# Both score maps of a differential attention at once, each on half the rows of TensorE's array

## The chip, the core and the metric

The kernel runs on one NeuronCore of a Trainium2 chip. Its engines work side by side, each through its own list of instructions: TensorE (PE) multiplies matrices, and its weight loads are listed apart as PEld; VectorE is DVE, ScalarE is ACT, GpSimd is POOL; SyncE (SP) issues most of the loads. The metric is the device time of one execution in microseconds (us). Before the change three runs gave 3132.48, 3139.52 and 3141.57 us; the median is 3139.52 us.

TensorE multiplies a stationary operand, loaded into the array beforehand (up to 128 rows by 128 columns), with a moving operand that streams through it one column after another. The rows of the array are the index that is summed over. Every matrix product of this kernel loads its own stationary operand; the trace lists that load (LDWEIGHTS) and the product (MATMUL) apart. Products add up in PSUM.

## The reference

One layer of a decoder for a prompt of 2048 tokens and for 8 sample tokens: a normed input projection; a pooling mixer and a differential attention side by side; an output projection; cross attention into 256 memory tokens; a gated feed-forward with a short convolution; a final norm. All is float32. The change is in the prompt's differential attention, four heads, where each head has two maps c of 64 dimensions:

```
s = jnp.einsum('bqhcd,bkhcd->bhcqk', q, k) * (DIFF_HD ** -0.5)          # DIFF_HD = 64
s = jnp.where(dist >= 0, s + bias, -jnp.inf)                             # bias: -slope of the head * distance
a = jax.nn.softmax(s, axis=-1)
w = a[:, :, 0] - lam * a[:, :, 1]                                        # the two maps
o = jnp.einsum('bhqk,bkhe->bqhe', w, v)
```

## The kernel before

**Precision.** TensorE takes its operands in fp32r, which keeps fewer bits than float32. So nearly every operand is split into a high and a low part (hi, lo), and a product is built from hi by hi, hi by lo and lo by hi, three products that accumulate in PSUM.

**Stages.** The prompt is cut into four chunks of 512 tokens (the last carries the 8 sample rows too). The work is written as a list of items; `weave` spreads one list among another by estimated times, and the framework that builds the program then sets the order of instructions on every engine, with semaphores for what depends on what. The attention of chunks 0 and 1 (`att01`) is woven into the input projection of chunks 2 and 3; the attention of chunks 2 and 3 (`att23`) is woven with the output projection, the cross attention of chunk 0 and some work on the memory. Feed-forward fills the rest of the program.

**Attention.** A `Unit` is one head's 128 queries, 64 units in all. Unit i of a head (0 to 15) has (i + 1) * 128 keys. They are taken in halves of at most 1024 keys, so units 0 to 7 have one half and units 8 to 15 two. `scores(c, hf)` handles one map and one half: it takes a PSUM tile of 1024 columns from a pool of two (`PA`), fills it by products of at most 512 columns (line 1057), and VectorE then reads it, adds the distances and keeps the running minimum (line 1068, tile T out of sc). ScalarE takes the exponentials (line 1075), `combine` and `combine2` form the difference of the maps (lines 1084 to 1092), `turn` transposes it on TensorE (line 1098, wT), and `av` multiplies it with the values (line 1109, O). The steps of three successive units are mixed: scores of unit i, combination of i - 1, transposes and values of i - 2.

**Operands of the scores.** `k_evac` splits a chunk's keys into kh and kl (128 rows each: 64 of map 0, 64 of map 1) and stores them in DRAM by map: for map c, the 64 rows of kh above the 64 rows of kl. `att_load` brings one such tile K[c][hf] of 128 rows for each map and half. `att_q` brings, for each map, the high and the low queries, each of them twice, in rows 0 to 63 and again in rows 64 to 127, by four loads. So one product over all 128 rows gives qh by (kh + kl), a second ql by (kh + kl): two products a map, four for both.

Of the kernel before, what the change touches and what calls it, by code (L numbers as in the profile page):

```python
# [20 lines left out]
P = 128  # L21
# [25 lines left out]
def tile_trunk_step(ctx: ExitStack, tc: tile.TileContext, a, o):  # L47
# [142 lines left out]
    def rstd_v(ss, p, n, scale, eps):  # L190
        """as rstd, on the vector engine alone: a first guess from the exponent's bits, and three steps of Newton's"""
        v_, y, t = Tn("rv"), tp.tile([P, 8], I32, tag="t", name="ri"), Tn("rt")
        v_, y, t = v_[:p, :n], y[:p, :n], t[:p, :n]
        V.tensor_scalar(v_, ss, scale, eps, ALU.mult, ALU.add)
        V.tensor_scalar(y, v_.bitcast(I32), 1, None, ALU.logical_shift_right)
        V.tensor_scalar(y, y, -1, 0x5F3759DF, ALU.mult, ALU.add)
        y = y.bitcast(F32)
        for _ in range(3):
            V.scalar_tensor_tensor(t, y, -0.5, v_, ALU.mult, ALU.mult)
            V.tensor_tensor(t, t, y, ALU.mult)  # L200
            V.scalar_tensor_tensor(y, t, 1.5, y, ALU.add, ALU.mult)
        return y
# [13 lines left out]
    def norm_steps(c, x, g0, name, done, spill=None, rs=None):  # L216
        """items that norm the chunk x (4 tiles, in place), spill x to DRAM, and split the result"""
# [63 lines left out]
    class Weight:  # L281
        """a weight tile of 1024 columns in k parts, as loaded or as its high and low parts"""
# [19 lines left out]
    def cols(name, c0):  # L302
        """n-tile of 128 columns of a [1024, N] weight: [128, 8 kt, 128]"""
        return lambda: Weight(a[name][0, :, c0:c0 + P].rearrange("(k p) n -> p k n", p=P), 8)
# [11 lines left out]
    def item(specs, fn, cost=0.0, lat=0.0):  # L316
        """a piece of work: the weight tiles that it takes, the tensor engine's time in it, and how long what
        follows it in its own list has to wait"""
        return (specs, fn, cost, max(lat, cost, 0.3))

    def steps(specs, fn, cost, n):
        """fn's work, a generator, as n items"""
        st = {}

        def part(i):
            def run(ws):
                if i == 0:
                    st["g"] = fn(ws)
                next(st["g"], None)
                if i == n - 1:  # L330
                    for _ in st["g"]:
                        pass
            return run

        return [item(specs if i == 0 else [], part(i), cost / n) for i in range(n)]

    def weave(main, extra, lo=0.0, hi=1.0):
        """extra's items spread over main's span [lo, hi], both kept in order, by their times"""
        tm, te = sum(i[2] for i in main) or 1.0, sum(i[3] for i in extra) or 1.0
        out, k, dm, de = [], 0, 0.0, 0.0  # L340
        for i in main:
            out.append(i)
            dm += i[2]
            while k < len(extra) and lo + (hi - lo) * (de / te) <= dm / tm:
                out.append(extra[k])
                de += extra[k][3]
                k += 1
        return out + extra[k:]

    def in_turn(parts):  # L350
        """each one's four parts (load, split, product, turn), the load ahead by one and the turn behind by one"""
        out = [parts[0][0]]
        for b, p in enumerate(parts):
            out += [q[0] for q in parts[b + 1:b + 2]] + [p[1]] + ([parts[b - 1][3]] if b else []) + [p[2]]
        return out + [parts[-1][3]]

    def merge(x, y):
        """x's and y's items in one list, as long as the longer of the two"""
        tx, ty = sum(i[3] for i in x), sum(i[3] for i in y)
        both_, n = [], max(tx, ty)  # L360
        for z, t in ((x, tx), (y, ty)):
            at = 0.0
            for i in z:
                both_.append((at / t, i))
                at += i[3]
        both_.sort(key=lambda e: e[0])
        ends = [e[0] for e in both_[1:]] + [1.0]
        return [i[:3] + ((end - at) * n,) for (at, i), end in zip(both_, ends)]
# [4 lines left out]
    def later(dt, fn, key=None):  # L373
        """fn is traced when dt more of the tensor engine's time has been, or when its key is needed"""
        pending.append((clock[0] + dt, fn, key))
# [20 lines left out]
    def drive(items):  # L396
        """runs items in order; the weights of later ones are loaded ahead[0] tiles before their use, and their high
        and low parts taken ahead[1] and ahead[2] tiles before it"""
# [23 lines left out]
    def proj(c, hs, w, name):  # L422
        """[128 n, tokens of chunk c] of an n-tile; hs = (hi, lo) of the chunk, w = (hi, lo) [128, 8, 128]"""
# [271 lines left out]
    def k_evac(c, h, view):  # L695
# [6 lines left out]
        for cc in range(2):  # L702
            for z, t in enumerate((kh, kl)):
                ST.dma_start(k_d[c // 2][h][cc, z * HD:(z + 1) * HD, t0:t0 + CH], f(t[cc * HD:(cc + 1) * HD, :CH]))
# [228 lines left out]
    def sample_av(b):  # L933
# [27 lines left out]
        def fn3(_):  # L961
# [5 lines left out]
            # row (z, h) of head h's columns  # L967
# [43 lines left out]
    def att_load(h, nhf, old):  # L1011
        def fn(_):
            K = [[None, None] for _ in range(2)]
            Vt = [None, None]
            for hf in range(nhf):
                for c in range(2):
                    K[c][hf] = H("K", F32R)
                    SY.dma_start(f(K[c][hf][:, :1024]), k_d[hf][h][c])
# [5 lines left out]
    def att_q(qc, h):  # L1024
        def fn(_):
            q = [H("Q", F32R) for _ in range(2)]
            for c in range(2):
                for half in range(2):
                    SY.dma_start(f(v3(q[c], 2)[half * HD:(half + 1) * HD]),
                                 q_d[qc][:, h, c * HD:(c + 1) * HD, :].rearrange("z p t -> p z t"))  # L1030
# [3 lines left out]
    class Unit:  # L1034
        """a head's 128 queries"""
# [11 lines left out]
        def scores(self, c, hf):  # L1047
            def fn(_):
                if c == 0 and hf == 0:
                    self.l, self.mn = Tn("l"), [Tn("mn"), Tn("mn")]  # L1050
                Q, K = att["Q", self.qc, self.h], att[self.key][0]
                k0, m = self.halves[hf]
                ps = PA("sc")
                pc = [(0, m)] if m <= 512 else [(0, m // 2), (m // 2, m // 2)]
                for j, (c0, w) in enumerate(pc):
                    for z in range(2):
                        PE.matmul(ps[:, j * 512:j * 512 + w], v3(Q[c], 2)[:, z, self.t * P:(self.t + 1) * P],  # L1057
                                  K[c][hf][:, c0:c0 + w], start=z == 0, stop=z == 1)
                tl = H("T")
                d0 = 1920 - self.i * P + k0  # L1060
                if len(pc) == 1:
                    pin, out, din = ps[:, :m], tl[:, :m], Dt[:, d0:d0 + m]
                else:
                    pin = ps[:, :].rearrange("p (a b) -> p a b", a=2)[:, :, :m // 2]
                    out = tl[:, :m].rearrange("p (a b) -> p a b", a=2)
                    din = Dt[:, d0:d0 + m].rearrange("p (a b) -> p a b", a=2)
                mn = self.mn[c]
                V.tensor_tensor_reduce(out, pin, din, -SLOPE[self.h], 3.0e38 if hf == 0 else mn[:, 0:1], ALU.add, ALU.min,  # L1068
                                       mn[:, hf:hf + 1])
                self.T[c].append(tl)  # L1070
                last = len(self.halves) - 1
                if hf == last:
                    for g, (_, mg) in enumerate(self.halves):
                        tg = self.T[c][g]
                        S.activation(tg[:, :mg], tg[:, :mg], AF.Exp, bias=mn[:, last:last + 1], scale=-1.0,  # L1075
                                     accum_out=self.l[:, 2 * g + c:2 * g + c + 1])
            return item([], fn, self.halves[hf][1] / 512 * 0.43)
# [34 lines left out]
        def a_steps(self):  # L1112
            return [self.scores(c, hf) for c in range(2) for hf in range(len(self.halves))]
# [38 lines left out]
    def att_items(qcs):  # L1152
# [10 lines left out]
        for i in range(len(units) + 2):  # L1163
# [4 lines left out]
            if A:  # L1168
                k = 2 if len(A) > 2 else 1
                seq = A[:k] + B[:1] + A[k:] + B[1:]  # L1170
# [140 lines left out]
    sco = cp.tile([P, KT, NS], F32, name="sco")  # L1311

    def both(key, name, src, write):
        """items: rows of the samples (high parts over low ones) times a [1024, 1024] weight, by its quarters"""
# [66 lines left out]
    def sc_av(b):  # L1381
# [25 lines left out]
        def fn3(_):  # L1407
# [5 lines left out]
            # row (z, h) of head h's columns, which are tiles 2 h and 2 h + 1  # L1413
# [106 lines left out]
    def tail_down(nt, xx):  # L1520
        """the last chunk's squares and first half of its rows, as its tiles become final"""
# [128 lines left out]
    def raw_open(_):  # L1650
        """the distances' table gives its place to weights as they are loaded"""
# [52 lines left out]
```

## Time and profile before

| | us |
|---|---|
| median of the three runs | 3139.52 (3132.48 to 3141.57) |
| profiled execution, first to last instruction (span) | 3141.1 |
| TensorE busy with products (PE) | 3018.7 (96%) |
| TensorE busy with weight loads (PEld) | 2611.7 (83%) |
| VectorE busy | 2011.3 (64%) |
| ScalarE busy | 1403.9 (45%) |
| GpSimd busy | 530.8 (17%) |
| products of the scores, 640 | 172.9 busy, 386 ns each on the mean |

The profile is one execution of its own, listed by its span alone; no time around the span is shown for it. Busy times of TensorE need care: a product's listed duration goes from its start to the end of its results, and several are in the pipe at once, so what a product costs the engine is read from the distance between the starts of two neighbours, not from its duration. A weight load is listed beside the product that runs before it.

The scores run from 296 to 1043 us of the span. In that stretch TensorE is shared with the input projection (z, v), the output projection (wo), cross attention (S, vo) and the attention's own transposes and values.

### The profile page before, as it was taken

The numbers are of one execution on the slowest core, as the hardware profiler recorded it, in microseconds if no ns is written. First come the engines' busy times: TensorE is split into PE (matmuls) and PEld (weight loads), VectorE is DVE, ScalarE is ACT, GpSimd is POOL, SyncE is SP. The second block draws the span as 40 slices with busy tenths as digits, with TensorE's granted clock in tenths as the row PEclk, the third lists the DMA queues.
The fourth block names the chain that finished last, engine by engine and source line by source line (L and its number), as shares of the span: only waits on it lengthen the run. The fifth ranks groups of instructions, "written<-read, shape, count | busy, mean of one in ns | idle before, by whom it ended". The sixth has DMA issues, their size and how long they took to land.

```text
span 3141.1 us, 45513 instructions
## 1 busy us (share of the span) xinstructions
PE 3018.7 (96%) x17694; PEld 2611.7 (83%) x17694; DVE 2011.3 (64%) x3241; ACT 1403.9 (45%) x2214; POOL 530.8 (17%) x905
## 2 busy tenths in 40 slices
PE   7999999998999988999999999999999999999998
PEld 6789899887898877887777878887787777899998
DVE  5715654568667577757775546647767667866566
ACT  4625444446655444534443334534444344443342
POOL 0134234211111135302400000000013100010000
PEclk9999999899999999999999999999999999999999
DMA  8646356442632635434536432342455544343321
GB/s 272 189 150 226 102 163 190 148 138 64 206 107 85 212 117 161 157 117 137 161 105 213 148 109 94 112 150 92 163 175 207 166 144 169 121 142 96 94 81 71
DMA packets 378204, 451.98 MB, mean 144 GB/s; under 512 B 18321, under 2 KB 292248, under 8 KB 377972
## 3 DMA queue, kind: packets, MB, share of 16 engines
q1 hardware_dynamic: 336925, 349.29, 35.1%
q0 software_dynamic: 27264, 89.03, 8.2%
q10 hardware_dynamic: 13798, 10.76, 1.1%
q8 instruction: 139, 2.28, 0.3%
q14 instruction: 78, 0.63, 0.1%
HBM read 364.57 MB, written 84.85 MB: 143 GB/s over the span
## 4 chain that ended last, share of the span: by engine, by line
PE 82%; DVE 9%; DMA 3%; issue 2%; ACT 2%; POOL 1%; SPq 0%; DVEq 0%; ACTq 0%; POOLq 0%
PE up L429 19%; PE down L1503 13%; PE up L432 10%; PE z L443 8%; PE wo L443 6%; PE O L1109 3%; PE sc L1057 3%; DVE wlo L297 2%; PE vo L94 2%; PE vo L96 2%; PE vo L95 2%; PE S L94 2%; PE S L96 1%; PE S L95 1%; PE wT L1098 1%
## 5 line engine op out<-in xcount | busy, mean ns | idle before, releaser
L297 DVE TENSOR_TENSOR wlo<-wraw,whi 128x1024 fp32r<-128x1024 f32 x432 | 529.6, 1240 | 71.0 <-ACT whi L294 62.4
L429 PE MATMUL up<-h3hi,wlo 128*128 128x512 f32 (+1 forms) x1760 | 562.6, 352 | 7.7 <-ACT cc L1457 3.4
L429 PE MATMUL up<-h3hi,whi 128*128 128x512 f32 (+1 forms) x1760 | 559.6, 351 | 0.0
L294 ACT CAST whi<-wraw 128x1024 fp32r<-128x1024 f32 x432 | 443.1, 1048 | 238.4 <-DMA wraw<-in_w_up_dram 58.1
L1503 PE MATMUL down<-act,whi 128*128 128x512 f32 (+1 forms) x1760 | 449.8, 353 | 13.7 <-DVE xf L1510 13.2
L1463 DVE SCALAR_TENSOR_TENSOR cc<-Uf,vec,cc 128x512 f32<-128x512 f32 x176 | 135.0, 767 | 365.3 <-ACT cc L1457 353.3
L432 PE MATMUL up<-h3lo,whi 128*128 128x512 f32 (+1 forms) x1760 | 357.6, 349 | 0.0
L429 PEld LDWEIGHTS up<-h3hi,wlo 128*128 128x128 f32 x1760 | 308.4, 189 | 55.5 <-ACT cc L1457 3.9
L1456 ACT COPY Uf<-up 128x512 f32<-128x512 f32 (+1 forms) x176 | 103.6, 589 | 554.9 <-PE up L432 543.7
L429 PEld LDWEIGHTS up<-h3hi,whi 128*128 128x128 f32 x1760 | 308.4, 189 | 44.9
L1503 PEld LDWEIGHTS down<-act,whi 128*128 128x128 f32 x1760 | 293.5, 189 | 61.5 <-DVE xf L1510 17.4
L432 PEld LDWEIGHTS up<-h3lo,whi 128*128 128x128 f32 x1760 | 285.5, 188 | 46.8
L1503 PE MATMUL down<-act,wlo 128*128 128x512 f32 (+1 forms) x880 | 280.7, 352 | 3.5 <-DVE wlo L297 3.5
L1462 POOL COPY halo<-Uf 128x2 f32<-128x2 f32 x176 | 54.3, 308 | 1355.5 <-ACT Uf L1456 1355.3
L1510 DVE TENSOR_TENSOR xf<-xf,down 128x512 f32<-128x512 f32 (+1 forms) x308 | 206.7, 683 | 76.5 <-PE down L1503 75.0
L1075 ACT ACTIVATE T<-T,mn 128x1024 f32<-128x1024 f32 (+4 forms) x192 | 171.9, 897 | 128.3 <-DVE mn L1068 122.5
L1057 PE MATMUL sc<-K,Q 128*128 128x512 f32 (+5 forms) x640 | 172.9, 386 | 12.9 <-DVE mn L1068 12.6
L1068 DVE CUSTOM_DVE_ANT_0 T<-sc,Dt 128x1024 f32<-128x1024 f32 (+7 forms) x128 | 125.8, 985 | 86.1 <-PE sc L1057 83.5
L1503 PEld LDWEIGHTS down<-act,wlo 128*128 128x128 f32 x880 | 154.5, 189 | 29.3 <-DVE wlo L297 5.9
L443 PE MATMUL z<-h1hi,wlo 128*128 128x512 f32 (+1 forms) x480 | 158.4, 363 | 4.4 <-DVE pps L668 4.4
L1087 POOL TENSOR_SCALAR T<-T,rc 128x1024 f32<-128x1024 f32 (+4 forms) x96 | 92.4, 970 | 371.1 <-DVE rc L1085 194.4
L443 PE MATMUL z<-h1hi,whi 128*128 128x512 f32 (+1 forms) x480 | 153.8, 353 | 0.0
(420 smaller groups left out, 5994.2 us busy)
## 6 DMA issues: line engine op xcount, KB each, us to landing
wraw<-in_w_up_dram SPq DMA_DIRECT2D x176, 512.0 KB
wraw<-in_w_down_dram SPq DMA_DIRECT2D x88, 512.0 KB
wraw<-in_w_in_dram SPq DMA_DIRECT2D x32, 512.0 KB
Q<-q_d SPq DMA_DIRECT2D x64, 256.0 KB
wraw<-in_w_out_dram SPq DMA_DIRECT2D x32, 512.0 KB
wraw<-m_d SPq DMA_DIRECT2D x32, 512.0 KB
wraw<-vo_d SPq DMA_DIRECT2D x32, 512.0 KB
K<-k_d SPq DMA_DIRECT2D x24, 512.0 KB
```

Source lines behind the costliest of these rows:

```text
L94: PE.matmul(out, lh, rl, start=first, stop=False)
L294: S.copy(self.hi[:, :1024], self.raw[:, :1024])
L297: V.tensor_tensor(self.lo[:, :1024], self.raw[:, :1024], f(self.hi[:, :1024]), ALU.subtract)
L429: PE.matmul(out, w[wi][:, kt, :], kslice(hi, kt, c0, n), start=kt == 0 and wi == 1, stop=False)
L432: PE.matmul(out, w[0][:, kt, :], kslice(lo, kt, c0, n), start=False, stop=kt == KT - 1)
L443: PE.matmul(out, w[wi][:, kt, :], kslice(z, kt, c0, n), start=i == 0, stop=i == 3 * KT - 1)
L1057: PE.matmul(ps[:, j * 512:j * 512 + w], v3(Q[c], 2)[:, z, self.t * P:(self.t + 1) * P], K[c][hf][:, c0:c0 + w], start=z == 0, stop=z == 1)
L1068: V.tensor_tensor_reduce(out, pin, din, -SLOPE[self.h], 3.0e38 if hf == 0 else mn[:, 0:1], ALU.add, ALU.min, mn[:, hf:hf + 1])
L1075: S.activation(tg[:, :mg], tg[:, :mg], AF.Exp, bias=mn[:, last:last + 1], scale=-1.0, accum_out=self.l[:, 2 * g + c:2 * g + c + 1])
L1463: V.scalar_tensor_tensor(cc[:, :CH], U[:, 1:1 + CH], vc(CWT + FT + nt), cc[:, :CH], ALU.mult, ALU.add)
L1503: PE.matmul(out, ws[p][wi][:, nt, :], act[:, z + c0:z + c0 + n], start=st_ and p == 0, stop=en and p == 1)
L1510: V.tensor_tensor(sv(xx, c), sv(xx, c), view, ALU.add)
```

## The change

The scores of both maps are now one item, `scores(hf)`. It takes both PSUM tiles of the pool at once. For each piece of at most 512 columns it makes six products in place of four: low keys by high queries, high keys by high queries, high keys by low queries, each for map 0 (array rows 0 to 63) and map 1 (array rows 64 to 127) in alternation. Low by low, which the products over 128 rows included, is left out. Keys and queries stay as they are split: K[z][hf] holds the high (z = 0) or the low (z = 1) keys of both maps in 128 rows, and the query tile Q holds each row once. `k_evac` stores with two issues instead of four, `att_q` loads with one instead of four. The item's estimated time, which `weave` uses, is 0.7 us per 512 columns for both maps, where it was 0.43 for each. With half as many items, `att_items` cuts the list after the first one.

```diff
 def k_evac(c, h, view):
-        for cc in range(2):
-            for z, t in enumerate((kh, kl)):
-                ST.dma_start(k_d[c // 2][h][cc, z * HD:(z + 1) * HD, t0:t0 + CH], f(t[cc * HD:(cc + 1) * HD, :CH]))
+        for z, t in enumerate((kh, kl)):
+            ST.dma_start(k_d[c // 2][h][z, :, t0:t0 + CH], f(t[:, :CH]))
...
 def att_load(h, nhf, old):
-                for c in range(2):
-                    K[c][hf] = H("K", F32R)
-                    SY.dma_start(f(K[c][hf][:, :1024]), k_d[hf][h][c])
+                for z in range(2):
+                    K[z][hf] = H("K", F32R)
+                    SY.dma_start(f(K[z][hf][:, :1024]), k_d[hf][h][z])
...
 def att_q(qc, h):
-            q = [H("Q", F32R) for _ in range(2)]
-            for c in range(2):
-                for half in range(2):
-                    SY.dma_start(f(v3(q[c], 2)[half * HD:(half + 1) * HD]),
-                                 q_d[qc][:, h, c * HD:(c + 1) * HD, :].rearrange("z p t -> p z t"))
+            q = H("Q", F32R)
+            SY.dma_start(f(v3(q, 2)), q_d[qc][:, h].rearrange("z p t -> p z t"))
...
-        def scores(self, c, hf):
+        def scores(self, hf):
-                ps = PA("sc")
+                ps = [PA("sc"), PA("sc")]
                 pc = [(0, m)] if m <= 512 else [(0, m // 2), (m // 2, m // 2)]
                 for j, (c0, w) in enumerate(pc):
-                    for z in range(2):
-                        PE.matmul(ps[:, j * 512:j * 512 + w], v3(Q[c], 2)[:, z, self.t * P:(self.t + 1) * P],
-                                  K[c][hf][:, c0:c0 + w], start=z == 0, stop=z == 1)
-                tl = H("T")
+                    for zq, zk in ((0, 1), (0, 0), (1, 0)):
+                        for c in range(2):
+                            rows_ = slice(c * HD, (c + 1) * HD)
+                            PE.matmul(ps[c][:, j * 512:j * 512 + w], Q[rows_, zq, self.t * P:(self.t + 1) * P],
+                                      K[zk][hf][rows_, c0:c0 + w], start=zk == 1, stop=zq == 1)
...
-            return item([], fn, self.halves[hf][1] / 512 * 0.43)
+                for c in range(2):
+                    tl = H("T")
...
+            return item([], fn, self.halves[hf][1] / 512 * 0.7)
...
 def a_steps(self):
-            return [self.scores(c, hf) for c in range(2) for hf in range(len(self.halves))]
+            return [self.scores(hf) for hf in range(len(self.halves))]
...
 def att_items(qcs):
-                k = 2 if len(A) > 2 else 1
-                seq = A[:k] + B[:1] + A[k:] + B[1:]
+                seq = A[:1] + B[:1] + A[1:] + B[1:]
```

What stands on TensorE in the new program is not simply the order of that loop, because the framework orders the instructions. Two places show it. In these rows a tile's number tells the PSUM tile: an item of the new program has two sc tiles, the first for map 0 (array rows 0 to 63), the second for map 1 (rows 64 to 127).

TensorE in the first part of the attention (head 0, unit 3, one piece of 512 columns), before; z is the input projection of chunk 3:

```order
L443 MATMUL z_3022<-h1hi_2822,whi_2655 128x260 x2
L1057 MATMUL sc_3057<-K_2641,Q_2647 128x512 x2
L443 MATMUL z_3022<-h1hi_2882,wlo_2659 128x260 x2
...
L96 MATMUL pool_3084<-phi_3010,pws_921 128x512
L1057 MATMUL sc_3091<-K_2643,Q_2648 128x512 x2
L443 MATMUL z_3022<-h1lo_2764,whi_2655 128x260 x4
```

The same place in the new program:

```order
L443 MATMUL z_3008<-h1hi_2742,whi_2635 128x260 x2
L1057 MATMUL sc_3027<-K_2627,Q_2631 128x512
L1057 MATMUL sc_3027<-K_2625,Q_2631 128x512 x2
L443 MATMUL z_3008<-h1hi_2742,wlo_2639 128x260 x2
L443 MATMUL z_3008<-h1hi_2742,whi_2635 128x260 x2
L443 MATMUL z_3008<-h1hi_2802,wlo_2639 128x260 x2
L443 MATMUL z_3008<-h1hi_2802,whi_2635 128x260 x2
L1057 MATMUL sc_3028<-K_2627,Q_2631 128x512
L1057 MATMUL sc_3028<-K_2625,Q_2631 128x512 x2
```

The three products of map 0 stand by themselves, then come products of the projection, and only then the three of map 1.

TensorE in the second part (head 0, unit 14, halves of 1024 and 896 columns), before; wo is the output projection of chunk 0:

```order
L1057 MATMUL sc_6780<-K_5768,Q_6431 128x512 x4
L443 MATMUL wo_6745<-mixhi_6267,wlo_6563 128x512
...
L1098 MATMUL wT_6809<-ident_75,T_6552 128x128 x4
L1057 MATMUL sc_6816<-K_5774,Q_6431 128x448 x4
L443 MATMUL wo_6745<-mixlo_6254,whi_6495 128x512 x2
...
L1098 MATMUL wT_6832<-ident_75,T_6552 128x128 x4
L1057 MATMUL sc_6878<-K_5770,Q_6432 128x512 x4
L1057 MATMUL sc_6905<-K_5776,Q_6432 128x448 x3
```

The same unit in the new program, its first half:

```order
L443 MATMUL wo_6818<-mixhi_6299,whi_6547 128x512
L1057 MATMUL sc_6844<-K_5798,Q_6471 128x512
L1057 MATMUL sc_6845<-K_5798,Q_6471 128x512
L1057 MATMUL sc_6844<-K_5796,Q_6471 128x512
L1057 MATMUL sc_6845<-K_5796,Q_6471 128x512
L1057 MATMUL sc_6844<-K_5796,Q_6471 128x512
L1057 MATMUL sc_6845<-K_5796,Q_6471 128x512
...
L443 MATMUL wo_6818<-mixhi_6306,wlo_6620 128x512
```

Here the two maps alternate, twelve products for two pieces, between products of the output projection that use all 128 rows. Over the whole program, before has 640 score products in 171 runs that other products separate; the new one has 960 in 125 runs. Taken two by two along these runs, 344 pairs of neighbours are of different maps, and 272 products have no neighbour of the other map left. Counting every place on TensorE at which the number of array rows in use (32, 64 or 128) differs from that of the product ahead, before has 64 such changes and the new program 313. A change from map to map within a run, where 64 rows are in use on both sides, is not among these; there are 607 of those.

## Rows read from the trace of the kernel before

**Rows 1.** The page: busy time of the engines; chain that ended last, by engine.

```profile
PE 3018.7 (96%) x17694; PEld 2611.7 (83%) x17694; DVE 2011.3 (64%) x3241; ACT 1403.9 (45%) x2214; POOL 530.8 (17%) x905
PE 82%; DVE 9%; DMA 3%; issue 2%; ACT 2%; POOL 1%; SPq 0%; DVEq 0%; ACTq 0%; POOLq 0%
```

**Rows 2.** Stretch of attention: length, busy PE, PEld, DVE, ACT, POOL, clock, DMA.

```profile
295.00:1043.00 748.00, 711.67 (x4757) 639.55 (x4756) 474.10 (x967) 394.12 (x791) 169.64 (x233) 0.97 0.43 134
```

**Rows 3.** Waits of TensorE, 295 to 1045 us: total us, times, longest.

```profile
PE sc L1057 <- DVE mn L1068: 12.6, 13, 2.6
...
PEld sc L1057 <- DVE mn L1068: 20.7, 24, 3.0
```

**Rows 4.** Groups by shape, score products: columns, count, busy us, mean ns, idle before.

```profile
L1057 PE MATMUL sc<-K,Q 128*128 128x512 f32 x352 | 108.3, 424 | 8.0 <-DVE mn L1068 7.7
L1057 PE MATMUL sc<-K,Q 128*128 128x384 f32 x96 | 23.4, 353 | 0.0
L1057 PE MATMUL sc<-K,Q 128*128 128x448 f32 x64 | 16.7, 380 | 0.5 <-DVE mn L1068 0.5
L1057 PE MATMUL sc<-K,Q 128*128 128x320 f32 x64 | 12.3, 313 | 0.0
L1057 PE MATMUL sc<-K,Q 128*128 128x256 f32 x32 | 7.8, 330 | 0.0
L1057 PE MATMUL sc<-K,Q 128*128 128x128 f32 x32 | 6.4, 283 | 4.4 <-DVE mn L1068 4.4
```

**Rows 5.** Timeline of products: start us, length us (of xcount merged), line, tile.

```profile
617.22 0.40 PE L443 MATMUL wo<-mixhi,whi 128*128 128x512 f32 x1
617.46 0.40 PE L443 MATMUL wo<-mixhi,wlo 128*128 128x512 f32 x1
...
786.98 1.06 PE L1109 MATMUL O<-V,wT 128*128 128x128 f32 x8
...
789.55 0.28 PE L96 MATMUL M<-mkvT,wqlo 128*128 128x256 f32 x1
789.67 0.28 PE L94 MATMUL M<-mkvT,wqhi 128*128 128x256 f32 x1
...
1004.91 1.09 PE L1057 MATMUL sc<-K,Q 128*128 128x512 f32 x4
...
1011.03 1.17 PE L1057 MATMUL sc<-K,Q 128*128 128x512 f32 x4
```

**Rows 6.** Timeline of weight loads around products on 64 rows (wTs), feed-forward.

```profile
1397.24 1.59 PEld L432 LDWEIGHTS up<-h3lo,whi 128*128 128x128 f32 x7
1399.19 0.96 PEld L925 LDWEIGHTS wTs<-comb,ar 64*128 64x128 f32 x8 [0.36 <-issue]
...
1400.42 0.19 PEld L94 LDWEIGHTS vo<-Alo,whi 128*128 128x128 f32 x1
```

**Rows 7.** Timeline of products at the same place.

```profile
1398.64 0.63 PE L432 MATMUL up<-h3lo,whi 128*128 128x512 f32 x2
...
1400.11 0.38 PE L926 MATMUL wTs<-comb,ar 64*128 64x32 f32 x2
...
1400.76 0.39 PE L95 MATMUL vo<-Ahi,whi 128*128 128x512 f32 x1
```

**Rows 8.** Timeline of weight loads where products on 16 rows begin.

```profile
2659.51 0.57 PEld L1428 LDWEIGHTS scxT<-ident,sx 16*128 16x128 f32 x8 [0.37 <-issue]
```

**Rows 9.** Timeline between the two parts of the attention, products and VectorE.

```profile
603.00 2.50 PE L1057 MATMUL sc<-K,Q 128*128 128x512 f32 x6 [0.53 <-DVE mn L1068]
606.40 2.50 PE L1057 MATMUL sc<-K,Q 128*128 128x512 f32 x6 [0.90 <-DVE mn L1068]
...
605.11 1.23 DVE L1068 CUSTOM_DVE_ANT_0 T<-sc,Dt 128x1024 f32<-128x1024 f32 x1 [0.86 <-PE sc L1057]
```

**Rows 10.** DMA issues: destination, source, queue, count, KB each.

```profile
Q<-q_d SPq DMA_DIRECT2D x64, 256.0 KB
...
k_d<-kh POOLq DMA_DIRECT2D x32, 128.0 KB
```

More of the change, by code (lines that the diff above doesn't have):

```diff
@@ L1045, in __init__ @@
             self.wt = {}
-        def scores(self, c, hf):
+        def scores(self, hf):
             def fn(_):
-                if c == 0 and hf == 0:
+                if hf == 0:
                     self.l, self.mn = Tn("l"), [Tn("mn"), Tn("mn")]
-                Q, K = att["Q", self.qc, self.h], att[self.key][0]
+                Q, K = v3(att["Q", self.qc, self.h], 2), att[self.key][0]
                 k0, m = self.halves[hf]
-                ps = PA("sc")
+                ps = [PA("sc"), PA("sc")]
@@ L1054, in fn @@
                 pc = [(0, m)] if m <= 512 else [(0, m // 2), (m // 2, m // 2)]
                 for j, (c0, w) in enumerate(pc):
-                    for z in range(2):
-                        PE.matmul(ps[:, j * 512:j * 512 + w], v3(Q[c], 2)[:, z, self.t * P:(self.t + 1) * P],
-                                  K[c][hf][:, c0:c0 + w], start=z == 0, stop=z == 1)
-                tl = H("T")
-                d0 = 1920 - self.i * P + k0
[L1061 to L1070, printed above, removed]
-                last = len(self.halves) - 1
[L1072 to L1076, printed above, removed]
@@ new lines, in fn @@
+                for c in range(2):
+                    tl = H("T")
+                    if len(pc) == 1:
+                        pin, out, din = ps[c][:, :m], tl[:, :m], Dt[:, d0:d0 + m]
+                    else:
+                        pin = ps[c][:, :].rearrange("p (a b) -> p a b", a=2)[:, :, :m // 2]
+                        out = tl[:, :m].rearrange("p (a b) -> p a b", a=2)
+                        din = Dt[:, d0:d0 + m].rearrange("p (a b) -> p a b", a=2)
+                    mn = self.mn[c]
+                    V.tensor_tensor_reduce(out, pin, din, -SLOPE[self.h], 3.0e38 if hf == 0 else mn[:, 0:1], ALU.add, ALU.min,
+                                           mn[:, hf:hf + 1])
+                    self.T[c].append(tl)
+                    if hf == last:
+                        for g, (_, mg) in enumerate(self.halves):
+                            tg = self.T[c][g]
+                            S.activation(tg[:, :mg], tg[:, :mg], AF.Exp, bias=mn[:, last:last + 1], scale=-1.0,
+                                         accum_out=self.l[:, 2 * g + c:2 * g + c + 1])
```

## The prediction

> **What bounds the kernel now.** I read the page first: TensorE is busy for 96% of the span and carries 82% of the chain that ended last [rows 1]. Next, the stretch in which the scores run: from 295 to 1043 us TensorE is busy for 711.7 of 748 us, while VectorE has 474 us of work, ScalarE 394, GpSimd 170 and the DMA engines a share of 0.43 [rows 2]. So what counts is TensorE's time in this stretch, and other engines only where it waits for them. The list of its waits puts most of them at the scores, and none at a load of K or Q: 12.6 us in 13 waits of products and 20.7 us in 24 of their weight loads, all for VectorE's reading of an earlier PSUM tile [rows 3].
>
> **What a product costs.** Durations overlap, so I take the distance between starts. With 512 columns it is 0.23 to 0.24 us (617.22 to 617.46), with 256 columns 0.12 (789.55 to 789.67), with 128 columns (1.06 - 0.28) / 7 = 0.11 [rows 5]. The last is not half of the second: below some 240 columns the pace is that of the weight loads, 0.11 each. On the line between 256 and 512 columns I put 320 at 0.144, 384 at 0.173 and 448 at 0.202. By the counts of [rows 4] the scores of before take 352 x 0.23 + 96 x 0.173 + 64 x 0.202 + 64 x 0.144 + 32 x 0.118 + 32 x 0.112 = 127.1 us of TensorE, 0.199 for the mean product. This is the time of the engine, not the 172.9 us listed as busy.
>
> **Term 1, the products.** 640 become 960. Nothing in the trace shows two products on different halves of the array, so the price has two ends. If a product on 64 rows takes the engine as one on 128 does, as those on 64 rows in the feed-forward do at 0.11 a piece [rows 6, 7], it is 127.1 x 1.5 = 190.7: +63.6 us. If each product of map 1 ran entirely beside one of map 0, it is half of that, 95.3: -31.8 us. I expect the halves to overlap, since two such products share no array row, no partition of their operands and no PSUM tile; what they share is the stream of weight loads. But they can overlap only where they are neighbours. The order has 344 neighbouring pairs and 272 products alone. A pair takes the longer of one product and two loads (0.22): 88 of the 160 pieces have 512 columns (0.23), the others 0.22, so 0.2255 on the mean and 77.6 us for 344. The 272 take 0.199 each, 54.1 us. Sum 131.7: **+4.6 us**. Where the change was to save a quarter, its order gives the quarter back. Without the load floor it would be 616 x 0.199 = 122.6, or -4.5.
>
> The Trainium skill ("TensorE: Matmul & The Clock Gate", Part 3, row and column tiling) says that products on different row groups start some 4 ns apart, which is the -4.5 end, and no row here shows it. The same section says that a weight load overlaps a running product only on other rows of the array. By it each of the 272 lone products would also pay its load, 272 x 0.11 = 30 us more. The trace differs: full-height loads run under full-height products, which is how 512 columns come out at 0.23 and not 0.34 [rows 5], so I leave that out of the sum.
>
> **Term 2, changes of height.** TensorE now goes from products on 128 rows to products on 64 and back for every run of scores. The trace has this step in the feed-forward. Going in, the last product on 128 rows starts at 1398.64 + 0.23 = 1398.87 [rows 7], and the next could start at 1399.10. Its weight load, which otherwise runs ahead under the product before (the seven loads from 1397.24 follow one another at 0.23), starts only at 1399.19, after 0.36 us in which the loader stood idle for nothing that the profile names [rows 6]. With 0.11 for the load the product starts at 1399.30, 0.20 late. Going out, the last product on 64 rows starts at 1400.11 + 0.11 = 1400.22 [rows 7] and the next could follow at 1400.33; the load comes at 1400.42 [rows 6], and since the second product after it starts at 1400.76, 0.23 behind the first [rows 7], the first starts at 1400.53, again 0.20 late. The step onto 16 rows at 2659.51 shows the same 0.37 us of idle loader [rows 8]. The order counts 313 such changes against 64: 249 x 0.20 = **+49.8 us**, all on the bounding engine.
>
> Part of it was paid before. Some runs of scores began with a load that had waited: four products of 512 columns take 1.17 us in place of 1.09 [rows 5], in 21 of the 39 such runs. For half of 125 runs at 0.09 this is **-5.6 us**. And where TensorE stands for VectorE anyway, the engine empties meanwhile: 37 waits [rows 3] x 0.09 = **-3.3 us**.
>
> **Term 3, PSUM tiles.** An item takes both tiles of the pool, so map 0 of the next item waits until VectorE has read the first tile and map 1 until it has read the second, 1.23 us each for 1024 columns [rows 9]; behind the waiting product stand wT, O, wo and z on TensorE. Before, one tile was free while the other was read. Between two items the order mostly has several us of other products, more in the first part than in the second, where some twenty places have less than one reading's time. If the 33 us of waits [rows 3] grew by a third, +11. Against it, between the two parts TensorE and VectorE now alternate (four products, a reading, 3.4 us a map from 603.00 to 606.40 [rows 9], at the lower clock, where they follow at 0.43); two maps together are 6 x 0.43 + 2 x 1.23 = 5.0 in place of 6.8, for two or three pairs -5. I take **+2**, from -5 to +11.
>
> **Transfers and the rest, 0.** Q comes by 16 loads of 512 KB instead of 64 of 256 KB, and kh and kl each go out by 16 stores instead of 32 [rows 10]. They are issued by SP and by GpSimd, which is busy for 170 of 748 us [rows 2]; a unit's Q is asked for one unit ahead (748 / 64 = 11.7 us), and no wait of TensorE names it, so nothing shows. If that cover were missing the change would gain by it, not lose. VectorE's two readings come back to back instead of apart; the low parts of weights behind them are ready early enough that TensorE does not wait for them in this stretch. VectorE, ScalarE and GpSimd compute what they did. The estimates that weave the lists change by 20% for one kind of item; this moves work that TensorE does anyhow.
>
> **Sum.** 4.6 + 49.8 - 5.6 - 3.3 + 2 = +47.5 us on the profiled execution's span of 3141.1, so 3188.6. That execution lies 1.6 above the median of the three runs, and the profile gives nothing around its span; on the median's level I forecast **3187 us**, 1.5% slower. With the ends of terms 1 to 3 near the middle this case covers 3165 to 3205.
>
> **Rivals.**
> *The halves do not overlap.* The change does not do what it says: 63.6 + 49.8 - 5.6 - 3.3 + 2 = +106.5, 3246 us. For it: the only products on 64 rows that the trace shows go at the pace of whole ones. Against it: nothing that they share but the loads.
> *The change of height costs little here, and the kernel becomes faster.* The price of 0.20 is read where the step stands alone. If inside the attention the idle half of the array let the load run ahead, the term would vanish: -4.5 (products without a load floor) - 5.6 - 5 (pairs between the parts) = -15, 3124 us. It decides at (15 - 9) / 249 = 0.024 us a change for faster by over 0.3%, and at 15 / 249 = 0.06 for not slower. Against it: two places show it, one of them in both directions, with 0.36 and 0.37 us of idle loader.
> *Between the two,* half the price and the better products: -4.5 + 24.9 - 5.6 - 3.3 - 5 = +6.5, 3146, which is no change.
> *Every change from map to map empties the engine as a change of height does:* 607 x 0.20 = 121 more and no overlap, about 3367. No row shows a change of place at the same height. The Trainium skill ("TensorEngine Tiling (Array Packing)", Key Properties) says that changing the tiling mode drains the engine and changing the tile does not; by that rule this rival falls, and the 0.20 of term 2 is what the trace agrees with.
>
> **Chances.** My forecast 0.58; no overlap 0.18; cheap change of height 0.12; between 0.08; emptied at each map 0.04. For this kernel 0.3%, 9.4 us, is about what a measurement can tell from no change. Faster is the third, 0.12; no change the fourth, 0.08; slower the rest, 0.80. The range of 8 in 10 leaves out most of the faster case below and the last rival above, and reaches past 3246: 3132 to 3255.
>
> **What would show it.** In the new profile: LDWEIGHTS of sc with an idle loader of about 0.3 us ahead of each run, and again after it, put down to no engine; 250 times. Alternating products with two starts in 0.23 us (overlap) or 0.46 (none); lone runs at 0.23. TensorE's busy share in the stretch not lower, the stretch some 48 us longer, and everything outside it as before. It is wrong if the loads of a run's first product start under the product before it, if waits for VectorE at the scores pass 50 us, or if the stretch gets shorter.

## The result and the profile after

The changed kernel takes 3186.72 us (median of four runs, 3177.83 to 3188.20), where before took 3140.55 us beside it: 1.0155 of before, with a 95% interval of 1.0132 to 1.0178. It is 46 us slower; 3187 was forecast.

Two lines of the page of the changed kernel, the busy times and the chain by engine, answer to [rows 1]:

```profile
PE 3053.9 (96%) x18014; PEld 2610.3 (82%) x18014; DVE 2008.5 (63%) x3241; ACT 1403.1 (44%) x2214; POOL 513.1 (16%) x873
PE 80%; DVE 10%; ACT 3%; issue 3%; DMA 2%; POOL 1%; SPq 0%; DVEq 0%; POOLq 0%; ACTq 0%
```

Products are 320 more (18014 against 17694) and busy time of products is 35 us more, but the weight loads, of which there are as many more, are busy for 2610 us as before. "issue" has grown by a share of 1 in 100 of the chain: time in which an engine waits for nothing that the profile names.

The three stretches of the changed kernel, before, in and behind the attention (columns as in [rows 2]; the scores now end at 1082.6 us):

```profile
0.00:295.00 295.00, 271.02 (x1579) 235.34 (x1580) 144.61 (x237) 133.85 (x218) 66.85 (x146) 0.97 0.62 210
295.00:1088.00 793.00, 746.17 (x5060) 636.89 (x5059) 473.83 (x967) 388.90 (x785) 155.99 (x216) 0.97 0.35 114
1088.00:3186.50 2098.50, 2036.75 (x11379) 1738.05 (x11377) 1390.07 (x2038) 880.37 (x1212) 290.30 (x511) 0.99 0.43 139
```

All of the loss lies in the attention: 793 us in place of the 748 of [rows 2], with VectorE's work unchanged (473.8 and 474.1 us). What follows took 2098 us in either kernel. TensorE's granted clock is 0.97 on the mean in both stretches. From the first score product to the last it is 0.5 (1.2 GHz, the lower level) for 37.5 us before and for 44.4 us now; if all of these 7 us more went to products, which go at about half the pace there [rows 9], they would cost some 3.5.

How a run of scores stands in the new kernel: first the weight loads, then the products, between transposes (wT) and the work on the memory (VO). In brackets is the idle time ahead of the row.

```profile
824.81 0.91 PEld L1099 LDWEIGHTS wT<-ident,T 128*128 128x128 f32 x8
825.88 1.22 PEld L1057 LDWEIGHTS sc<-K,Q 64*128 64x128 f32 x12 [0.17 <-issue]
827.47 0.19 PEld L94 LDWEIGHTS VO<-wlo,mkvT 128*128 128x128 f32 x1 [0.36 <-issue]
```

```profile
824.91 1.04 PE L1099 MATMUL wT<-ident,T 128*128 128x128 f32 x8
825.88 1.65 PE L1057 MATMUL sc<-K,Q 64*128 64x512 f32 x12
827.47 0.51 PE L94 MATMUL VO<-wlo,mkvT 128*128 128x512 f32 x1
827.81 0.39 PE L95 MATMUL VO<-whi,mkvT 128*128 128x512 f32 x1
```

Read it as in [rows 6, 7]. The last transpose starts at 824.91 + 1.04 - 0.27 = 825.68, so the next product could start at 825.79; its load begins at 825.88 and takes 0.11, so it starts at 825.99: 0.20 late. Twelve products of 512 columns then end their streaming 6 x 0.23 = 1.38 us later, at 827.37: each pair cost one product. The product behind them starts at 827.81 - 0.23 = 827.58: 0.21 late. The run saves 0.46 us over the eight products of before (8 x 0.23 = 1.84) and pays 0.41 for its two changes of height. Of the 125 runs, 41 have twelve products and four have more (17, 24, 24 and 35). The other 80 are shorter, and a shorter run by itself saves less than its two changes cost.

The first run of the attention (six products of 128 columns), loads and then products, shows what a pair pays for its loads:

```profile
296.62 0.41 PEld L1057 LDWEIGHTS sc<-K,Q 64*128 64x128 f32 x6 [0.37 <-issue]
```

```profile
296.62 0.55 PE L1057 MATMUL sc<-K,Q 64*128 64x128 f32 x6
```

Less the first load (0.11) and the last product's length (0.27), 0.17 of the 0.55 us are left for two steps from pair to pair, some 0.1 each, not the 0.22 of two loads one behind the other that the forecast took as floor. The loads of the two halves run side by side: six take 0.41 us, where one behind the other they would take 5 x 0.11 + 0.19 = 0.74.

To add up the stretch I took the starts of all products on TensorE from the first to the last score product, in this kernel and in the experiments. Each product is given its pace by columns (as under [rows 5]); what a score product behind another starts earlier than that is overlap; a change of height is 0.196 us, which is the median delay over the 124 steps onto 64 rows and over the 125 steps back alike; the remainder is what is left: TensorE standing idle, and what products take longer at the lower clock. In us:

| kernel | score products one by one | overlap | changes of height | remainder | sum against before | measured against before |
|---|---|---|---|---|---|---|
| before | 127.7 | -0.9 | 4: 0.8 | 61.1 | | |
| changed | 191.5 | -69.7 | 253: 49.6 | 64.6 | +47 | +46 (ratio 1.0155) |
| new items only | 127.7 | -1.0 | 4: 0.8 | 77.8 | +17 | +21 (1.0071) |
| full height | 191.5 | -1.4 | 4: 0.8 | 62.1 | +64 | +65 (1.0204) |
| maps in turn | 191.5 | -50.0 | 241: 47.2 | 65.6 | +66 | +69 (1.0217) |
| second on 64 | 127.7 | -1.2 | 644: 126.2 | 30.7 | +95 | +101 (1.0315) |
| three by three | 191.5 | -65.5 | 259: 50.8 | 61.1 | +49 | +60 (1.0193) |
| fewer alone | 191.5 | -80.8 | 247: 48.4 | 80.8 | +51 | +55 (1.0169) |

Each row is one execution. That of before is the one at 3141.57 us; beside the experiments before took 3131.6 to 3133.9 us. By the same reckoning the trace of the run with before's items and another weaving estimate (3126.29 us, below) has a remainder some 10 us smaller than before's here, and against it every sum would be some 10 us larger. So the remainder, and the sums with it, are good to some 10 us; products, overlap and changes of height do not depend on this.

The waits of TensorE for VectorE at the scores, 295 to 1090 us, products and weight loads, answer to [rows 3]:

```profile
PE sc L1057 <- DVE mn L1070: 11.5, 11, 4.7
PE O L1110 <- ACT wT L1101: 7.1, 8, 1.9
```

```profile
PEld sc L1057 <- DVE mn L1070: 17.0, 19, 4.8
PEld O L1110 <- ACT wT L1101: 12.6, 18, 2.1
PEld sc L1057 <- issue: 10.7, 45, 0.4
```

The loads of the values (O) in the kernel before, 295 to 1045 us:

```profile
PEld O L1109 <- ACT wT L1100: 5.9, 9, 1.9
```

At the scores the waits for VectorE are no longer than before; at the values the loads wait 12.6 us for ScalarE's copies of the transposes, where it was 5.9. New are the waits that are put down to no engine ("issue"): 45 at the scores, and with those of all other loads 130 of them, 41 us together, against 3 with 3.3 us before.

### The profile page after: what moved, and what is told of

Same layout as the page of the kernel before. It is cut to its first block, busy times and chain, and to the rows that moved or that the text cites. A ratio compares the mean times of both kernels' runs of the same rounds, so it can differ in the third digit from the quotient of the medians.

```text
span 3186.5 us, 45964 instructions
## 1 busy us (share of the span) xinstructions
PE 3053.9 (96%) x18014; PEld 2610.3 (82%) x18014; DVE 2008.5 (63%) x3241; ACT 1403.1 (44%) x2214; POOL 513.1 (16%) x873
## 4 chain that ended last, share of the span: by engine, by line
PE 80%; DVE 10%; ACT 3%; issue 3%; DMA 2%; POOL 1%; SPq 0%; DVEq 0%; POOLq 0%; ACTq 0%
PE up L429 19%; PE down L1503 12%; PE up L432 9%; PE z L443 8%; PE wo L443 5%; PE O L1110 3%; PE sc L1057 3%; DVE wlo L297 2%; PE vo L94 2%; PE vo L96 2%; PE vo L95 2%; PE S L94 1%; PE S L96 1%; PE wT L1099 1%; PE S L95 1%
## 5 line engine op out<-in xcount | busy, mean ns | idle before, releaser
L1057 PE MATMUL sc<-K,Q 64*128 64x512 f32 (+5 forms) x960 | 160.0, 389 | 11.6 <-DVE mn L1070 11.5
L1110 PE MATMUL O<-V,wT 128*128 128x128 f32 x1088 | 153.5, 286 | 8.2 <-ACT wT L1101 7.1
L1110 PEld LDWEIGHTS O<-V,wT 128*128 128x128 f32 x1088 | 141.6, 200 | 18.6 <-ACT wT L1101 12.6
```

What stands on the lines that cost most here:

```text
L1057: PE.matmul(ps[c][:, j * 512:j * 512 + w], Q[rows_, zq, self.t * P:(self.t + 1) * P], K[zk][hf][rows_, c0:c0 + w], start=zk == 1, stop=zq ...
L1110: PE.matmul(O[:, self.t * P:(self.t + 1) * P], self.wt[g][:, (j % 4) * P:(j % 4 + 1) * P], v3(Vt[j // 8], 8)[:, j % 8, :], start=j == 0, s ...
```

## The experiments

Beside them before took 3131.6 to 3133.9 us, 7 to 9 us less than in the first comparison, so ratios are compared. "Theory" in the texts is that each product not overlapped costs 0.199 us and each change of height 0.196.

**The new items alone.** `k_evac`, `att_load` and `att_q` as before; `scores(hf)` as in the change, but

```diff
-                    for zq, zk in ((0, 1), (0, 0), (1, 0)):
+                    for z in range(2):
                         for c in range(2):
-                            PE.matmul(ps[c][...], Q[rows_, zq, ...], K[zk][hf][rows_, c0:c0 + w], ...)
+                            PE.matmul(ps[c][...], v3(Q[c], 2)[:, z, ...], K[c][hf][:, c0:c0 + w], ...)
```

> The kernel before with the new items alone: both maps in one item, both PSUM tiles taken at once, the new weaving estimate, but the four products on 128 rows with the old operands. 640 products, no added change of height (64, as before), 127 runs of scores. Theory (price is in the changes of height): 3140 us, within 10 of before. Rival (the pairing of the PSUM tiles and the other order of the work cost the time): 3165 to 3190.

Measured: 3155.24 us against 3133.89, ratio 1.0071 (1.0054 to 1.0088). Slower by 21 us, where the theory had at most 10 and the rival 25 to 50. The theory falls short here: the new items have a price of their own. Its waits in the stretch, products and then weight loads:

```profile
PE sc L1059 <- DVE mn L1072: 16.2, 15, 7.2
PE O L1112 <- ACT wT L1103: 7.2, 12, 1.9
```

```profile
PEld sc L1059 <- DVE mn L1072: 23.6, 24, 7.3
PEld O L1112 <- ACT wT L1103: 12.8, 18, 2.3
```

The remainder in the table is 16.7 us more than before's, products and changes being equal, and 13 us more than that of the changed kernel, which has the same items. That the changed kernel hides most of this price, because VectorE and ScalarE catch up while TensorE pays for its changes of height, is a reading that no run shows by itself.

**Full height.** The change with each product over all 128 rows, map 0 first, and an order edge that holds an item's first product until VectorE has read the last tile of the item before it (a helper `behind` adds it):

```diff
-                    for zq, zk in ((0, 1), (0, 0), (1, 0)):
-                        for c in range(2):
-                            rows_ = slice(c * HD, (c + 1) * HD)
...
+                prev = None
+                for j, c0, w, zq, zk, c in [(j, *p, *z, c) for c in (0, 1) for j, p in enumerate(pc) for z in ((0, 1), (0, 0), (1, 0))]:
+                    rows_ = slice(0, P)
+                    i = PE.matmul(...)      # as before the edit
+                    if prev is not None:
+                        behind(i, prev)
+                    elif "read" in att:
+                        behind(i, att["read"], mybir.DependencyClass.Sync)
+                    prev = i
...
+                    att["read"] = V.tensor_tensor_reduce(...)      # as before the edit
```

> The new kernel with every one of its 960 products on all 128 rows, map 0's products first and map 1's behind them, the first product of an item held until VectorE has read the last tile of the item before (each score then sums over both maps: the values are not the attention's). No overlap, no added change of height (64 in the order). Theory, 0.199 us a product and 0.196 us a change: 320 more products than before, +63.7, so 3204 us (3195 to 3215). Rival (64-row products are what is slow, not the changes): near before.

Measured: 3198.79 us, ratio 1.0204 (1.0187 to 1.0221), +65 where +63.7 was reckoned, which is the pace of 320 more products with nothing overlapped and no change of height. It is no clean test of that pace: the new items, which cost 21 us by themselves, and the order edge are in this run too, and yet its remainder in the table is only 1 us above before's. The rival (near before) falls.

**Maps in turn.** As the last, but `rows_ = slice(c * HD, (c + 1) * HD)`.

> The same order as the run on full height, but each product on its map's 64 rows: map 0's products first and then map 1's, so few neighbours are of different maps (92 pairs, 776 alone) and the order has 301 changes of height. Theory: 868 slots of 0.199 against 640 of before, +45.4, and 237 changes, +46.5: 3232 us (3222 to 3245), so 50 above the new kernel and 28 above the run on full height. Rival (no overlap in the new kernel either): as the new kernel, 3187. Rival (changes free): 3186, 18 below the run on full height.

Measured: 3202.73 us, ratio 1.0217 (1.0200 to 1.0234): 4 us above the run on full height, with intervals that overlap, where the theory had 28 above and the rival that changes are free 18 below. Both miss, and the trace shows why. The same half of one unit, twelve products of 512 columns in which map 1's six stand behind map 0's six, first on full height, then on 64 rows, each in its own kernel:

```profile
706.86 3.01 PE L1060 MATMUL sc<-K,Q 128*128 128x512 f32 x12
```

```profile
711.41 2.23 PE L1060 MATMUL sc<-K,Q 64*128 64x512 f32 x12
```

The second took 0.8 us less, though no two neighbours but those in the middle are of different maps. The first three products start 0.23 apart, then two streams of starts run 0.115 apart, and the last three are 0.23 apart again: map 1's first product starts ahead of map 0's fourth, and the two maps run side by side from there to map 0's sixth. That also excludes the third forecast, no overlap in the new kernel. Overlap was 50.0 us in the whole, not the 18 of 92 pairs. With that the sum is 14.7 (products) + 46.4 (changes) + 4.5 (remainder) = 66, and 69 was measured.

**Three by three.** To test that by itself: the change with its two inner loops exchanged.

```diff
-                    for zq, zk in ((0, 1), (0, 0), (1, 0)):
-                        for c in range(2):
+                    for c in range(2):
+                        for zq, zk in ((0, 1), (0, 0), (1, 0)):
```

> The new kernel with the two inner loops exchanged: for each piece the three products of map 0, then the three of map 1, so that a product's neighbour of the other map stands three places behind it. The order has 319 changes of height (313 in the new kernel), 182 neighbouring pairs and 596 products alone. If TensorE takes products strictly in order: 778 slots of 0.199 against 616, so +32, 1.0255 of before, 3220 on the level of the first comparison. If a product of the other half may start ahead of up to three that stand before it, as the starts in the run with the maps in turn suggest: some 575 slots, -8, so 1.013 of before, 3180.

Measured: 3191.53 us, ratio 1.0193 (1.0175 to 1.0212), between the two. The order has 182 neighbouring pairs, the trace 298 pairs of score products that start within 60 ns of each other, and overlap is 65.5 us where strict order would have left some 36. Six products of 384 columns of the same unit, in the changed kernel (maps alternate), here (three of map 0, then three of map 1), and on full height:

```profile
299.55 0.79 PE L1057 MATMUL sc<-K,Q 64*128 64x384 f32 x6
```

```profile
298.60 0.80 PE L1057 MATMUL sc<-K,Q 64*128 64x384 f32 x6
```

```profile
298.30 1.20 PE L1060 MATMUL sc<-K,Q 128*128 128x384 f32 x6
```

The first two are the same. So a product on the free half does start ahead of three that stand before it; strict order is excluded by the starts. The ratio is higher than the changed kernel's, with intervals that just meet; the table, good to some 10 us, accounts for +49 of its +60, and what the rest is stays open.

**The second product on 64 rows.** The price of the change of height inside the attention, without any overlap: the kernel before with

```diff
                     for z in range(2):
-                        PE.matmul(ps[:, ...], v3(Q[c], 2)[:, z, ...], K[c][hf][:, c0:c0 + w], ...)
+                        r = slice(0, HD if z else P)
+                        PE.matmul(ps[:, ...], v3(Q[c], 2)[r, z, ...], K[c][hf][r, c0:c0 + w], ...)
```

> The kernel before with one edit: the second product of each piece (low queries) runs on rows 0 to 63 alone, which leaves out low queries by low keys. As many products, of the same columns, in the same order, none beside another, but 704 changes of height in the order in place of 64. Theory: 640 x 0.196 = +125, 3266 us (3245 to 3275; some fall into waits). Rival (a change costs only where it stands alone): below 3180.

Measured: 3234.99 us, ratio 1.0315 (1.0298 to 1.0332): +101 us. Its waits of weight loads, and the loads around one piece:

```profile
PEld sc L1058 <- issue: 105.3, 438, 0.4
...
PEld sc L1058 <- DVE mn L1069: 9.1, 11, 2.3
```

```profile
311.85 0.19 PEld L1058 LDWEIGHTS sc<-K,Q 128*128 128x128 f32 x1
312.40 0.18 PEld L1058 LDWEIGHTS sc<-K,Q 64*128 64x128 f32 x1 [0.36 <-issue]
312.83 0.30 PEld L443 LDWEIGHTS z<-h1lo,whi 128*128 128x128 f32 x2 [0.25 <-issue]
```

Between two products of one piece, of one map, the loader stands for 0.36 us as soon as the number of rows changes. The rival (cheap inside the attention) falls. 640 changes are 125 us of TensorE; 101 reach the time, a little below the 106 to 136 of the forecast. The remainder in the table is 30 us smaller: waits for other engines shrink (9.1 us of loads waiting for VectorE at the scores in place of 20.7), and some changes fall into waits. The net price here is 0.158 us a change, though each one on TensorE is 0.196.

**Map by map.** The new items alone, with the loop over maps outermost, to let VectorE read map 0 while TensorE fills map 1:

```diff
-                for j, (c0, w) in enumerate(pc):
-                    for z in range(2):
-                        for c in range(2):
+                for c in range(2):
+                    for j, (c0, w) in enumerate(pc):
+                        for z in range(2):
```

> The run with the new items alone (full height, four products), with the loop over maps outermost: map 0's tile is complete halfway through the item and VectorE can read it while TensorE fills map 1's. Theory (the new items cost because both tiles end together and are read one behind the other): half or more of the 21 us comes back, 1.001 to 1.004 of before. Rival (the cost is in the taking of both tiles at once or in the other weaving): as with the new items alone, 1.007.

Measured: 3149.57 us, ratio 1.0052 (1.0033 to 1.0071), against 1.0071 (1.0054 to 1.0088). The two intervals overlap, so this is inconclusive: some of the 21 us may come from the late end of both tiles, and this run does not settle how much.

**The estimates.** Before with `* 0.35` in place of `* 0.43`, and the change with `* 0.86` in place of `* 0.7`:

> The kernel before with the weaving estimate alone changed, 0.35 us per 512 columns and map (the new kernel's 0.7 for both) instead of 0.43. Theory (the estimate moves work and costs nothing; the new items cost by taking both tiles at once): within 0.3% of before. Rival (the new items' cost is the other weaving): 1.005 to 1.007 of before.

> The new kernel with the old estimate, 0.86 us per 512 columns for both maps. 307 changes of height, 353 pairs and 254 alone (313, 344, 272). Theory: 607 slots against 616, -2, and -1 for the changes: as the new kernel, 1.0145 of before within 0.3%. Rival (the weaving is what costs): 1.009 or less.

Measured: 3130.49 us, ratio 0.9992 (0.9983 to 1.0002), and 3182.53 us, ratio 1.0162 (1.0145 to 1.0179). The weaving estimates cost nothing in either. So the price of the new items is in the items: in taking both tiles at once, in the two readings one behind the other, or in the other cut of the list, which no run here parts.

**Fewer alone.** The change with the hold of the full-height run on an item's first product, the maps alternating, and no other order edges:

```diff
...
+                    if prev is None and "read" in att:
+                        behind(i, att["read"], mybir.DependencyClass.Sync)
...
```

> The new kernel with the first product of an item held until VectorE has read the last tile of the item before, so that both tiles are mostly free when a run begins: 409 neighbouring pairs and 142 products alone in the order (344 and 272), 307 changes of height (313). Theory: 551 slots against 616, -13, and -1 for the changes: 1.011 of before, 3173 on the level of the first comparison, if waits do not grow. Rival (the hold costs more than the pairs give): 1.0155 or more.

Measured: 3186.40 us, ratio 1.0169 (1.0152 to 1.0186), so the rival holds. Overlap rises by 11 us, where 13 were reckoned, and the remainder by 16. The wait at the scores has more than doubled against the changed kernel:

```profile
PE sc L1060 <- DVE mn L1076: 25.2, 12, 7.1
```

No run here beats before, and by the sums none with one item to a run does. If every item were one whole run with every product paired, the 96 runs would take 95.8 us of products (191.5 / 2) and 192 x 0.196 = 37.6 of changes, 133 against 127.6 of before, ahead of any wait for both tiles. Two or more items to a run would halve the changes or better; no run here tries that throughout, and the sum does not exclude it.

## Why the prediction was right

Its main step, term 2, is shown twice: 0.196 us a change read from the starts of 249 steps in the changed kernel (0.20 forecast; with the 249 added changes that the order counts it makes 48.8 us against 49.8), and by the run with the second product on 64 rows, which does nothing but add changes. The signs that the forecast named are there: two products in one product's time, a stretch 45 us longer (48 forecast) with everything behind it as it was, and an idle loader ahead of a run and behind it. Where 250 such places were forecast, the lists hold 130 waits put down to no engine; at 77 of the 253 changes in the stretch the loader stands for less than 0.15 us, and at others VectorE or ScalarE is named.

Term 1 was right in its argument, that the halves overlap, and too dear. The halves overlap, so the first rival falls, and they do so with no floor from the loads: products cost 126.8 us in before and 121.8 now, -5.0, where I took +4.6 and had named -4.5 as the price without the floor. Two wrong counts cancel inside that: pairs need not be neighbours, since a product may start ahead of up to three others, yet only 312 pairs of the changed kernel start within 60 ns of each other, against 344 in its order.

The terms for loads already waited for (-5.6), for waits that hide changes (-3.3) and for PSUM tiles (+2) made -6.9 together; the table's remainder grew by 3.5, give or take some 10. Here the sum came out right by luck: the product term was 10 us too high, and these three together came out some 10 too low. Term 3 put the pairing of the tiles at +2, from -5 to +11, and the new items by themselves cost 21 us, outside that range. In the changed kernel no run parts what they cost from the two credits.

One reading under these terms was wrong as well. The two lists of [rows 3] were added to 33 us in 37 waits, but all 13 waits of products stand at places that are among the 24 of the loads. TensorE waited at 24 places, at most 21 us; by that the credit is 24 x 0.09 = 2.2 in place of 3.3, and a third more of the waits is +7 in place of +11.

Of the rivals, no overlap and a cheap change are excluded by the traces. That a change from map to map empties the engine is excluded as well: of the 312 pairs of the changed kernel, 222 start at most 4 ns apart and 292 at most 10. The rule of the Trainium skill ("TensorEngine Tiling (Array Packing)", Key Properties), by which a change of the tile alone does not drain the engine, agrees with this. Transfers showed nothing, as forecast: no wait of TensorE in the changed kernel names a load of K or Q, though 8.4 MB less is moved.

## What to carry to other kernels

Two products on 64 rows each run in the time of one, but the step from 128 rows to 64 and back costs 0.2 us each way, so a run of such products has to save more than 0.4 us, here nearly two products of 512 columns (2 x 0.23), before it pays. Count the runs in the order that the program ends up with, not in the loop that was written: a stretch that shares the engine with full-height work is cut into many. And when a bounding engine gets slower or faster, read the waits of its neighbours again: 640 added changes cost 20% less than their sum, and TensorE's waits for others were shorter.

## What the runs showed of the hardware

Products on different halves of the array overtake one another: with three products of one half ahead of three of the other, the six take as long as if they alternated (0.80 and 0.79 us for 384 columns, 1.20 on full height), and with six ahead of six the second stream starts ahead of the first one's fourth product. Weight loads of the two halves run side by side, so pairs of 128 columns follow one another at some 0.1 us, no slower than single products on full height (0.11). Neither was in the forecast. And it is the change of rows that costs: in the kernel before, where TensorE goes onto at most 32 columns of the array at full height (30 steps) and back (38), the next product comes 4 and 1 ns late on the median.
